# Moving two small table loads from the store queue to the load queue, behind the first data tile

## The chip, the cores and the metric

The kernel runs on one core of a Trainium2 chip. The metric is the device time of one execution in microseconds (us), as a median of several executions. A profile of one execution gives a "span", from the first to the last of the program's own instructions, which is here about 1.8 us shorter than the time. Executions more than 1.5% above the fastest of the same kernel are called slow; the others are called fast.

A DMA is a transfer between the chip's main memory and the on-chip buffers. It is issued on a queue (the texts also say ring) and carried out in packets, one record each in the trace, by sixteen DMA engines that both queues of this kernel use. It has landed when a counter, its semaphore, has been raised sixteen times; "semaphore records" are the times of these raises.

A ratio below is the mean time of one kernel's fast runs over the mean of the other's fast runs of the same rounds. It is therefore not quite the ratio of the medians that are quoted next to it.

## The reference

A rotary embedding is applied to the first half of the last axis; the second half is passed through.

```python
# x: (16, 512, 16, 64) float32; cos, sin: (512, 32) float32
x1, x2 = x[..., :32], x[..., 32:]
c, s = cos[None, :, None, :16], sin[None, :, None, :16]      # only the first 16 columns are used
first  = x1[..., :16] * c - x1[..., 16:] * s
second = x1[..., :16] * s + x1[..., 16:] * c
out = concatenate([first, second, x2], axis=-1)
```

x is 33.55 MB and is read once and written once. Each table is 64 KB.

## The kernel before

x is cut into T = 8 tiles of 128 partitions by 8192 values (32 KB per partition, 4.19 MB per tile). A tile is loaded on the queue of the sync engine (SP), rotated in place by VectorE, and stored on the queue of ScalarE (ACT). Five x buffers exist, so load t+5 must wait until store t has landed. The two tables are loaded at the start on the store queue, into 64 partitions, and four small copies spread them over 128 partitions.

```python
    stage = const_pool.tile([PB, 2, K, HF], fp32)
    nc.scalar.dma_start(out=stage[:, 0].rearrange("p k j -> p (k j)"), in_=cosf)   # 64 KB
    nc.scalar.dma_start(out=stage[:, 1].rearrange("p k j -> p (k j)"), in_=sinf)   # 64 KB

    table = const_pool.tile([P, 2, K, 2, Q], fp32)
    for r in range(REP):            # 2
        for t in range(2):          # cos, sin
            nc.vector.tensor_copy(out=table[r * PB : (r + 1) * PB, t], in_=stage[:, t, ...])
    ...
    KC = 4
    for t in range(T):              # 8 tiles
        x_t = x_pool.tile([P, K, H, D], fp32)          # 5 buffers
        nc.sync.dma_start(out=x_t..., in_=xf[t])       # 4.19 MB
        for k0 in range(0, K, KC):                     # two halves
            ...
            nc.vector.tensor_mul(out=a_t[:], in0=x1, in1=c)
            nc.vector.tensor_mul(out=b_t[:], in0=x1, in1=s)
            nc.vector.tensor_sub(out=x1[:, :, :, 0:Q], ...)
            nc.vector.tensor_add(out=x1[:, :, :, Q:HF], ...)
        nc.scalar.dma_start(out=of[t], in_=x_t...)     # 4.19 MB
```

Of the kernel before, what the change touches and what calls it, by code (L numbers as in the profile page):

```python
# [1 line left out]

# [4 lines left out]


@with_exitstack
def kernel(  # L10
    ctx: ExitStack,
    tc: tile.TileContext,
    x: bass.AP,
    cos: bass.AP,
    sin: bass.AP,
    out: bass.AP,
):
    nc = tc.nc
    fp32 = mybir.dt.float32
    P = 128  # L20
    B, S, H, D = x.shape
    Q = D // 4
    HF = D // 2


    K = 8
    T = B * S // (P * K)
    PB = S // K
    REP = P // PB

    xf = x.rearrange("b s h d -> (b s h d)").rearrange("(t p f) -> t p f", t=T, p=P)
    of = out.rearrange("b s h d -> (b s h d)").rearrange("(t p f) -> t p f", t=T, p=P)
    cosf = cos.rearrange("(p k) j -> p (k j)", k=K)
    sinf = sin.rearrange("(p k) j -> p (k j)", k=K)

    const_pool = ctx.enter_context(tc.tile_pool(name="const", bufs=1))
    x_pool = ctx.enter_context(tc.tile_pool(name="xp", bufs=5))
    ab_pool = ctx.enter_context(tc.tile_pool(name="abp", bufs=1))

    stage = const_pool.tile([PB, 2, K, HF], fp32)  # L40
    nc.scalar.dma_start(out=stage[:, 0].rearrange("p k j -> p (k j)"), in_=cosf)  # L41
    nc.scalar.dma_start(out=stage[:, 1].rearrange("p k j -> p (k j)"), in_=sinf)


    table = const_pool.tile([P, 2, K, 2, Q], fp32)
    for r in range(REP):
        for t in range(2):
            nc.vector.tensor_copy(  # L48
                out=table[r * PB : (r + 1) * PB, t],
                in_=stage[:, t, :, 0:Q].unsqueeze(2).to_broadcast((PB, K, 2, Q)),  # L50
            )
    C = table[:, 0].rearrange("p k c j -> p k (c j)")
    Sn = table[:, 1].rearrange("p k c j -> p k (c j)")

    KC = 4
    for t in range(T):
        x_t = x_pool.tile([P, K, H, D], fp32)
        nc.sync.dma_start(out=x_t.rearrange("p k h d -> p (k h d)"), in_=xf[t])  # L58
        for k0 in range(0, K, KC):
            x1 = x_t[:, k0 : k0 + KC, :, 0:HF]  # L60
            c = C[:, k0 : k0 + KC].unsqueeze(2).to_broadcast((P, KC, H, HF))
            s = Sn[:, k0 : k0 + KC].unsqueeze(2).to_broadcast((P, KC, H, HF))
            a_t = ab_pool.tile([P, KC, H, HF], fp32)
            b_t = ab_pool.tile([P, KC, H, HF], fp32)
            nc.vector.tensor_mul(out=a_t[:], in0=x1, in1=c)  # L65
            nc.vector.tensor_mul(out=b_t[:], in0=x1, in1=s)  # L66
            nc.vector.tensor_sub(  # L67
                out=x1[:, :, :, 0:Q], in0=a_t[:, :, :, 0:Q], in1=b_t[:, :, :, Q:HF]
            )
            nc.vector.tensor_add(  # L70
                out=x1[:, :, :, Q:HF], in0=a_t[:, :, :, Q:HF], in1=b_t[:, :, :, 0:Q]
            )
        nc.scalar.dma_start(out=of[t], in_=x_t.rearrange("p k h d -> p (k h d)"))


# [1 line left out]
_INS = ['x', 'cos', 'sin']  # L77
_OUTS = [((16, 512, 16, 64), 'float32')]


# [23 lines left out]
```

## Time and profile before

| | before |
|---|---|
| time, median of the first 3 runs | 162.37 us (162.19 to 162.39) |
| span in the profile | 160.4 us |
| VectorE busy | 110.8 us (69%) |
| moved by DMA | 67.25 MB, mean 419 GB/s |
| one 32 KB packet on one DMA engine (packet records) | 1.213 us, on either queue |

The profile's page of the kernel before: span, busy time of VectorE (DVE), and strips of 40 slices of 4 us each, in which a digit is the busy share in tenths.

```profile
span 160.4 us, 155 instructions
DVE 110.8 (69%) x68; POOL 0.2 (0%) x4
DVE  0001599999999999999998799609995099940000
DMA  7999999999999999999999999999999999999993
DMA packets 2465, 67.25 MB, mean 419 GB/s; under 512 B 288, under 2 KB 416, under 8 KB 416
```

DMA is at 9 from the second slice to the last but one. VectorE is idle in the first three slices, has holes late, and is done four slices before the end. Sixteen engines at 32,768 B per 1.213 us move 432 GB/s, and 67.2 MB at 432 GB/s take 155.6 us. That is nearly the whole span.

The timeline of the kernel before (start us, duration us, engine and line, operation, count; in brackets the idle time before and what ended it; SPq and ACTq are the sequencers that issue DMAs):

```profile
0.73 0.54 ACTq L41 DMA_DIRECT2D stage<-in_cos_dram  x1
0.73 11.78 SPq L58 DMA_DIRECT2D x_t<-in_x_dram  x5
1.30 0.61 ACTq L42 DMA_DIRECT2D stage<-in_sin_dram  x1
...
12.19 0.59 DVE L48 COPY table<-stage 64x256 f32<-64x256 f32 x2 [12.19 <-DMA stage<-in_cos_dram]
17.67 0.59 DVE L48 COPY table<-stage 64x256 f32<-64x256 f32 x2 [4.90 <-DMA stage<-in_sin_dram]
18.29 2.29 DVE L65 TENSOR_TENSOR a_t<-x_t,table 128x2048 f32<-128x2048 f32 x1
...
32.14 0.35 ACTq L73 DMA_DIRECT2D out_dram<-x_t  x1
```

Two 64 KB loads issued at 0.73 and 1.30 us hold VectorE up until 12.19 and 17.67 us. X tile 0 landed at 13.62 us (semaphore records), so 18.29 us is 4.7 us later than the data would allow. This is what the change is after.

The waits of the kernel before (who waited for what: us in total, number of waits, longest):

```profile
DVE a_t L65 <- DMA x_t<-in_x_dram: 13.2, 3, 5.9
DVE table L48 <- DMA stage<-in_cos_dram: 12.2, 1, 12.2
DVE table L48 <- DMA stage<-in_sin_dram: 4.9, 1, 4.9
```

The chain of work that ended last, of the kernel before (start us, us, what), cut to its two long links:

```profile
59.83 34.11 DMA out_dram<-x_t
...
93.99 34.21 DMA x_t<-in_x_dram
```

A store takes 34 us from issue to landing, and the load that waits for its buffer takes 34 us more. One tile alone takes 9.7 us at 432 GB/s (4.19 MB / 432 GB/s); the rest is standing in queues that are never empty.

### The profile page before, as it was taken

What the parts mean: (1) busy time and instruction counts of PE and PEld (TensorE: products, weight loads), DVE (VectorE), ACT (ScalarE), POOL (GpSimd) and SP (SyncE); (2) the same over time, 40 slices, a digit from 0 to 9 for tenths busy, and PEclk for the clock granted to TensorE, in tenths of its full rate; (3) what the DMA queues carried; (4) which work ended last, traced back from release to release, by engine and by line L of the source; (5) the groups of instructions that cost most, each with busy time, mean ns of one, the idle gap of its engine ahead of it and who ended that gap; (6) DMA issues with size and microseconds to landing.
All of it is one profiled execution on the core that took longest, in us unless ns stands there. A gap on an engine that the chain in (4) does not pass through costs nothing.

```text
span 160.4 us, 155 instructions
## 1 busy us (share of the span) xinstructions
DVE 110.8 (69%) x68; POOL 0.2 (0%) x4
## 2 busy tenths in 40 slices
DVE  0001599999999999999998799609995099940000
POOL 0000000000000000000000000000000000000000
DMA  7999999999999999999999999999999999999993
GB/s 253 408 400 408 392 417 490 400 408 498 400 400 474 433 392 457 457 392 449 466 392 417 490 400 408 498 400 400 476 425 400 466 441 400 449 457 400 417 482 147
DMA packets 2465, 67.25 MB, mean 419 GB/s; under 512 B 288, under 2 KB 416, under 8 KB 416
## 3 DMA queue, kind: packets, MB, share of 16 engines
q1 hardware_dynamic: 1152, 33.55, 49.3%
q10 hardware_dynamic: 1312, 33.69, 48.7%
q14 instruction: 1, 0.01, 0.0%
HBM read 33.69 MB, written 33.55 MB: 419 GB/s over the span
## 4 chain that ended last, share of the span: by engine, by line
DMA 53%; DVE 30%; issue 4%; DVEq 1%; ACTq 0%; SPq 0%
DMA x_t<-in_x_dram 21%; DMA out_dram<-x_t 21%; DVE b_t L66 11%; DMA stage<-in_sin_dram 10%; DVE a_t L65 10%; DVE x_t L70 5%; DVE x_t L67 4%; DVEq L99 1%; ACTq L41 0%; DVE table L48 0%; SPq L58 0%; DVEq L65 0%
## 5 line engine op out<-in xcount | busy, mean ns | idle before, releaser
L65 DVE TENSOR_TENSOR a_t<-x_t,table 128x2048 f32<-128x2048 f32 x16 | 36.7, 2292 | 13.6 <-DMA x_t<-in_x_dram 13.2
L66 DVE TENSOR_TENSOR b_t<-x_t,table 128x2048 f32<-128x2048 f32 x16 | 36.5, 2284 | 0.0
L67 DVE TENSOR_TENSOR x_t<-a_t,b_t 128x1024 f32<-128x1024 f32 x16 | 19.6, 1226 | 0.6
L70 DVE TENSOR_TENSOR x_t<-a_t,b_t 128x1024 f32<-128x1024 f32 x16 | 19.5, 1218 | 0.0
L48 DVE COPY table<-stage 64x256 f32<-64x256 f32 x4 | 1.1, 287 | 17.1 <-DMA stage<-in_cos_dram 12.2
L88 POOL MEMSET const-bfloat16-1.0<- 128x1 bf16 x1 | 0.1, 102 | 0.0
L88 POOL MEMSET const-uint8-127<- 128x1 uint8 x1 | 0.1, 102 | 0.0
L88 POOL MEMSET const-float32-0.0<- 128x1 f32 x1 | 0.1, 99 | 0.2 <-issue 0.2
L88 POOL MEMSET const-float32-1.0<- 128x1 f32 x1 | 0.1, 99 | 0.0
## 6 DMA issues: line engine op xcount, KB each, us to landing
x_t<-in_x_dram SPq DMA_DIRECT2D x8, 4096.0 KB, 33.9
out_dram<-x_t ACTq DMA_DIRECT2D x8, 4096.0 KB, 31.3
stage<-in_cos_dram ACTq DMA_DIRECT2D x1, 64.0 KB, 11.4
stage<-in_sin_dram ACTq DMA_DIRECT2D x1, 64.0 KB, 16.3
```

The lines of the kernel that those rows point to most:

```text
L48: nc.vector.tensor_copy(out=table[r * PB : (r + 1) * PB, t], in_=stage[:, t, :, 0:Q].unsqueeze(2).to_broadcast((PB, K, 2, Q)),)
L65: nc.vector.tensor_mul(out=a_t[:], in0=x1, in1=c)
L66: nc.vector.tensor_mul(out=b_t[:], in0=x1, in1=s)
L67: nc.vector.tensor_sub(out=x1[:, :, :, 0:Q], in0=a_t[:, :, :, 0:Q], in1=b_t[:, :, :, Q:HF])
L70: nc.vector.tensor_add(out=x1[:, :, :, Q:HF], in0=a_t[:, :, :, Q:HF], in1=b_t[:, :, :, 0:Q])
L88: nc = _bacc.Bacc("TRN2", target_bir_lowering=False, num_devices=1)
L99: with _tile.TileContext(nc) as tc:
```

## The change

Its intent: load x tile 0 first, put the tables right behind it on the same queue, and so let VectorE begin as soon as tile 0 is there.

```diff
+    x_0 = x_pool.tile([P, K, H, D], fp32, name="x_t")
+    nc.sync.dma_start(out=x_0.rearrange("p k h d -> p (k h d)"), in_=xf[0])
+
     stage = const_pool.tile([PB, 2, K, HF], fp32)
-    nc.scalar.dma_start(out=stage[:, 0].rearrange("p k j -> p (k j)"), in_=cosf)
-    nc.scalar.dma_start(out=stage[:, 1].rearrange("p k j -> p (k j)"), in_=sinf)
+    nc.sync.dma_start(out=stage[:, 0].rearrange("p k j -> p (k j)"), in_=cosf)
+    nc.sync.dma_start(out=stage[:, 1].rearrange("p k j -> p (k j)"), in_=sinf)
 ...
     for t in range(T):
-        x_t = x_pool.tile([P, K, H, D], fp32)
-        nc.sync.dma_start(out=x_t.rearrange("p k h d -> p (k h d)"), in_=xf[t])
+        if t == 0:
+            x_t = x_0
+        else:
+            x_t = x_pool.tile([P, K, H, D], fp32, name="x_t")
+            nc.sync.dma_start(out=x_t.rearrange("p k h d -> p (k h d)"), in_=xf[t])
```

## The prediction

> **What bounds the kernel.** DMA, nearly from end to end. The page's DMA view gives 67.25 MB at a mean of 419 GB/s over the 160.4 us span; in its strip of 40 slices DMA stands at 9 in all but the first and last. In the packet records a 32 KB packet takes 1.213 us on either queue; 16 engines then move 432 GB/s, and 67.2 MB take 155.6 us. First packet 1.7 us, last 159.2: under 2 us is lost. VectorE is busy 110.8 us (69%). The chain of waits starts with 16.3 us of "DMA stage<-in_sin" and VectorE work, but from 59.8 us it is store, load: full queues.
>
> **What the change does.** The same bytes move. The two 64 KB table loads leave the store queue (ScalarE) for the load queue (SP), behind x tile 0. Before, cos was issued at 0.73 us and landed at 12.16, sin at 17.65, although a 1 KB packet itself takes 46 ns. The Trainium skill, "DMA: Bandwidth & Descriptors", section "Queues, rings and completion order", says each engine round-robins between queues at packet granularity. The trace agrees: 4 data packets and a completion per engine took 6.2 us (5.95 to 12.16), five turns of 1.24 us, each behind one 32 KB packet of x. In one ring behind x tile 0, the tables pass together.
>
> Costed: x tile 0 landed at 13.6 us with the tables taking turns; without them about 13.0. Both tables should land by about 13.3. Two copies (0.6 us), first multiply about 13.9 (before: 18.29). The sin copies now sit between the first two multiplies (by the order of instructions). First store issued at about 28.3 us instead of 32.14: VectorE gains about 4 us.
>
> **How much is critical.** Almost nothing. I replayed the transfers as two first-in-first-out queues that share 432 GB/s equally when both have work, five x buffers, 13.85 us of VectorE per tile. With the old start this gives the old landings within 1 us. With the start 4 us earlier, early stores take bandwidth from loads sooner: tile 3 lands at about 54 us (before 50.4), the last load at about 132 (before 128.2). The last store is issued at about 146 instead of 142.1, still about 2 us before the previous store has drained, so DMA never runs dry: the end stays at about 159.4. The early microseconds come back as VectorE waiting for x.
>
> Small terms: the table turns cost about 0.6 us of DMA throughput between 6 and 18 us (bytes by 20 us against 432 GB/s); small packets in a row in the load ring may cost as much, or up to 1 us.
>
> **Prediction:** 162.2 us, range 161.3 to 163.4 (8 in 10). Faster by over 2%: 0.02. Within 2%: 0.96. Slower by over 2%: 0.02.
>
> **What would show the steps.** Cos, sin and x tile 0 landing within 1 us of each other, at 12.5 to 14.5 us. First store near 28 us. DMA strip still 9 throughout. VectorE busy still about 110.8 us; its wait for the tables shrinks to about zero; its wait for x rises from 13.2 us in 3 waits to about 33 (13 before the first tile, then four of 4 to 6). Last load lands 3 to 5 us later, last store issued near 146 us, landing near 159.
>
> **What would make it wrong.** DMA running dry at the end, if the last load lands after about 134 us (up to 1.5 us slower); small packets stalling the load ring by microseconds; a changed reuse of DMA semaphores that delays a load; a rate that differs between pure and mixed traffic, since the pure-load stretch shortens.

## The result, and the profile after

| first measurement | before | after |
|---|---|---|
| median of all 6 runs | 162.28 us | 162.73 us |
| range | 162.16 to 162.77 | 162.20 to 175.38 |
| ratio of the fast runs | | 1.0005 (95%: 0.9981 to 1.003) |

The fast runs are the same. Two of the six runs of the changed kernel were slow (172.58 and 175.38 us), and its first profile fell into one of these. The profile shown here as "after" is therefore that of a second measurement of the identical kernel (after_again, 162.25 us, a fast run).

The page of the changed kernel in a fast run:

```profile
span 160.5 us, 154 instructions
DVE 110.8 (69%) x68; POOL 0.2 (0%) x4
DVE  0005999999999999957997099950999319993000
DMA  7999999999999999999999999999999999999993
DMA packets 2465, 67.25 MB, mean 419 GB/s; under 512 B 288, under 2 KB 416, under 8 KB 416
```

The DMA strip is the same, digit for digit. VectorE's strip has a 5 instead of a 1 in the fourth slice, where it starts, and its holes come earlier and are one more.

The timeline of the changed kernel in the same run:

```profile
0.73 0.36 SPq L41 DMA_DIRECT2D x_t<-in_x_dram  x1
1.14 0.53 SPq L44 DMA_DIRECT2D stage<-in_cos_dram  x1
1.72 0.58 SPq L45 DMA_DIRECT2D stage<-in_sin_dram  x1
...
13.65 0.59 DVE L51 COPY table<-stage 64x256 f32<-64x256 f32 x2 [13.65 <-DMA stage<-in_cos_dram]
14.27 2.29 DVE L71 TENSOR_TENSOR a_t<-x_t,table 128x2048 f32<-128x2048 f32 x1
16.48 0.58 DVE L51 COPY table<-stage 64x256 f32<-64x256 f32 x2
...
28.74 0.38 ACTq L79 DMA_DIRECT2D out_dram<-x_t  x1
```

The change does what it intends. X tile 0, cos and sin land at 13.38, 13.63 and 13.93 us, the first multiply starts 4.0 us earlier, and the first store goes out 3.4 us earlier (28.74 against 32.14; the sin copies now stand between the first two multiplies).

The waits of the changed kernel:

```profile
DVE a_t L71 <- DMA x_t<-in_x_dram: 20.3, 4, 6.1
DVE table L51 <- DMA stage<-in_cos_dram: 13.7, 1, 13.7
```

VectorE waited 12.2 + 4.9 = 17.1 us at the start before, and 13.7 us now: 3.4 us saved. It waited 13.2 us for later x tiles before, and 20.3 us now: 7.1 us lost. So VectorE ends its last tile 3.7 us later than before, and the kernel is not slower only because the store queue was still busy with the store before, as the landing times below show.

The chain of the changed kernel, the same two links:

```profile
56.44 33.63 DMA out_dram<-x_t
...
90.12 41.74 DMA x_t<-in_x_dram
```

The store is issued 3.4 us earlier and lands 3.9 us earlier, so the last load is issued 3.9 us earlier (90.12 against 93.99). But that load then takes 41.7 us instead of 34.2, because more of the load queue is still ahead of it: it lands at 131.86 us, 3.7 us **later** than before (128.20).

All of this is seen at once in the landing times, read from the semaphore records of the two traces (us):

```
                          before   after (fast)
first store issued         32.14      28.74
x tile 2 landed            33.43      34.49
x tile 3 landed            50.43      53.86
x tile 4 landed            69.78      73.20
x tile 7 landed (last)    128.20     131.86
last store issued         142.14     145.80
store before it landed    149.95     149.97
last store landed         159.59     159.61
```

Until the first store's packets (from 36.03 us before, from 32.39 us after), the load queue has the DMA engines alone, apart from the tables. From then on, as long as there are loads, the two queues share them about half each in the packet records of both traces (50% and 50% before, 51% and 49% after). A store that starts 3.4 us earlier takes its share from the loads about as much sooner. The order of the bytes changes; their sum and the rate do not.

### The profile page after: what moved, and what is told of

It is laid out like the page before. It is cut to its first block, busy times and chain, and to the rows that moved or that the text cites. A ratio compares the mean times of both kernels' runs of the same rounds, so it can differ in the third digit from the quotient of the medians.

```text
span 170.8 us, 154 instructions
## 1 busy us (share of the span) xinstructions
DVE 110.8 (65%) x68; POOL 0.2 (0%) x4
## 4 chain that ended last, share of the span: by engine, by line
DMA 57%; DVE 29%; issue 3%; DVEq 1%; SPq 0%
DMA out_dram<-x_t 25%; DMA x_t<-in_x_dram 24%; DVE b_t L72 10%; DVE a_t L71 9%; DMA stage<-in_cos_dram 7%; DVE x_t L76 5%; DVE x_t L73 4%; DVEq L105 1%; DVE table L51 0%; SPq L41 0%; SPq L64 0%; DVEq L71 0%
## 5 line engine op out<-in xcount | busy, mean ns | idle before, releaser
L51 DVE COPY table<-stage 64x256 f32<-64x256 f32 x4 | 1.1, 284 | 13.9 <-DMA stage<-in_cos_dram 13.9
```

## The experiments

Theory A is the one of the prediction: the transfers are a fixed 67.2 MB at about 432 GB/s, and VectorE's head start only moves stores ahead of loads. Four rivals are tested along with it: the head start is real and is eaten by the table packets in the load ring (B); an earlier start can never hurt (C); the start of VectorE is critical, microsecond for microsecond; the end of the kernel is bound by its last tile.

### after_again: the changed kernel once more

No edit.

> The changed kernel again, unedited, to get a profile of an undisturbed execution (the first one was of the slow state) and to count slow executions of both kernels. Theory A (the transfers are a fixed 67.2 MB at about 432 GB/s, and a head start of VectorE only reorders loads and stores): 162.0 to 162.6 us in fast runs, first store issued at 29 us, last load landing at 132 to 133, last store issued at 146 to 147, DMA never idle until 159. Rival B (the head start is real and is eaten by the table packets in the load ring): the same total, but x tiles 1 and 2 landing some 4 us later than before, and a DMA strip with a hole near 12 to 16 us.

Measured: fast runs 162.25 to 162.60 us, ratio 0.9997 (0.9982 to 1.0012), and one slow run of 168.55 in five. Its profile is the one shown above. X tile 1 landed at 23.50 us (before 23.73) and x tile 2 at 34.49 (33.43), so the 4 us that rival B expects to be lost between 12 and 35 us are not lost there. Each number of theory A came out within 1 us.

### no_tables: the tables' traffic taken away

```diff
-    nc.sync.dma_start(... in_=cosf)
-    nc.sync.dma_start(... in_=sinf)
-    for r in range(REP): ...tensor_copy(out=table[...], in_=stage[...])
+    nc.vector.memset(table[:], 1.0)          # wrong result on purpose
```

> The tables are filled with a constant by VectorE instead of being loaded (wrong result on purpose). First multiply at about 13.4 us, when x tile 0 lands. Theory A: only the table traffic goes, 0.3 us of bytes and up to 0.5 us of bubble: 0.3 to 0.8 us faster than before, 161.5 to 162.0. Rival B (table packets in the load ring eat about 4 us): 157.5 to 159 us.

Measured: 162.47 us, ratio 1.0005 (0.9992 to 1.0018). Rival B falls: without any table packets nothing is gained, and the 1.2 us found below is too little for its 4 us. But the expectation of A was missed as well, by 0.3 to 0.8 us. The packet records tell where that went. With each packet's bytes spread over its duration, DMA moved, in GB/s by stretches of 5 us (432 is full; rows and columns are our own sums):

```
us from start       5-10  10-15  15-20  20-25  25-30  30-35  35-40
before               427    396    419    431    432    432    433
after (fast)         433    389    432    432    432    427    434
no_tables            433    433    433    433    398    361    433
no_tables_warm       430    426    432    432    417    380    433
no_tables_delay      433    433    433    433    433    414    402
```

Before, the tables cost throughput in turns from 5 to 20 us; after, in one piece at 10 to 15 us: (432 - 389) x 5 us = 0.2 MB, or 0.5 us. Without tables this loss is gone. In its place load packets of 1.4 to 2.7 us instead of 1.213 appear from 28 to 33 us, about the time of the first store: (34 + 71) x 5 us = 0.5 MB, or 1.2 us. The saving (0.3 us of table bytes and 0.5 us of loss) was spent there.

### early and early_split: an even earlier start

```diff
+    # early: tables first, then x tile 0 in two half loads
     nc.sync.dma_start(... in_=cosf)
     nc.sync.dma_start(... in_=sinf)
-    nc.sync.dma_start(out=x_0..., in_=xf[0])
+    for k0 in range(0, K, 4):
+        nc.sync.dma_start(out=x_0[:, k0 : k0 + 4]..., in_=xf[0][:, k0 * H * D : (k0 + 4) * H * D])
 ...
+    # early_split: in addition the last tile's store in two halves, each as soon as it is computed
+            if t == T - 1:
+                nc.scalar.dma_start(out=of[t][:, k0 * H * D : (k0 + KC) * H * D], in_=x_t[:, k0 : k0 + KC]...)
```

> Tables at the head of the load queue and x tile 0 in two half loads, so that VectorE starts at 8 to 10 us and the first store goes out at about 24 us instead of 29. Theory A: the loads fall back further behind the stores, the last load lands at about 137, the last store is issued at about 151 while the store before has drained at 148.6: DMA is idle for 2.5 to 4 us and the kernel gets slower, 164.5 to 166.5 us. Rival C (an earlier start cannot hurt, at worst it is absorbed): 162.0 to 162.6 us or less.

> As early, and the store of the last tile goes out in two halves, the first as soon as its half is computed. Theory A: the hole before the last store is filled by the first half, back to 162.0 to 162.8 us. If early was slower for another cause than the hole at the end (the split load of x tile 0, the tables in front): no recovery, 164.5 or more.

Measured: early 166.95 us, ratio 1.0272 (1.0245 to 1.0298); early_split 163.79 us, ratio 1.0089 (1.0073 to 1.0106). Both lie above their ranges of theory A, by 0.5 and 1.0 us. Early missed on the side away from rival C. Early_split missed towards its rival (no recovery, 164.5 us or more): of the 4.5 us that early lost, 3.2 came back, so the hole at the end is most of the loss and not all of it. VectorE starts 4.7 us earlier than in the changed kernel (9.59 against 14.27), and the kernel becomes 2.7% slower than before. Rival C falls. The last load of early lands at 139.12 us and its last store is issued at 153.06, after the store before it had landed (151.20).

The windows view shows the hole (window, its length, busy time of VectorE and count, of GpSimd, the TensorE clock, DMA share, GB/s; a packet counts whole in the window in which it starts, so a share can be over 1). First the changed kernel in a fast run:

```profile
145.00:150.00 5.00, 0.77 (x1) 0.00 (x0) 1.00 1.03 446
150.00:155.00 5.00, 0.00 (x0) 0.00 (x0) 1.00 1.08 465
```

Then early:

```profile
145.00:150.00 5.00, 4.97 (x3) 0.00 (x0) 1.00 0.94 406
150.00:155.00 5.00, 2.99 (x3) 0.00 (x0) 1.00 0.24 105
```

Then early_split:

```profile
145.00:150.00 5.00, 4.97 (x4) 0.00 (x0) 1.00 1.00 433
150.00:155.00 5.00, 3.14 (x3) 0.00 (x0) 1.00 0.98 419
```

In early, DMA is at 24% from 150 to 155 us, while VectorE works on the last tile: nothing is left to move. The first half of the last store fills this hole in early_split and wins back 3.2 us. The 1.4 us that remain over before are the start: with the tables in front, DMA had moved 0.5 MB by 5 us instead of 1.0 MB (1.15 us), and packets were slow about the first store here too (0.8 us); the 0.5 us of the table loss are saved.

### behind_x1, behind_x2, behind_x3: a later start

The tables stand behind x tiles 0 to 1, 0 to 2, or 0 to 3 on the load queue.

```diff
     nc.sync.dma_start(out=x_0..., in_=xf[0])
+    nc.sync.dma_start(out=x_1..., in_=xf[1])        # behind_x1
+    nc.sync.dma_start(out=x_2..., in_=xf[2])        # behind_x2, with the line above
+    nc.sync.dma_start(out=x_3..., in_=xf[3])        # behind_x3, with both
     nc.sync.dma_start(... in_=cosf)
     nc.sync.dma_start(... in_=sinf)
```

> The change with one more x tile ahead of the tables: x tiles 0 and 1, then the tables. First multiply at about 24 us, ten later than in the changed kernel and six later than before. Theory A (VectorE's start is off the critical path within a band): 162.0 to 162.8 us, last load landing at about 123, last store issued at about 137, DMA never idle. A rival that takes the start of VectorE for critical (each us of start is a us of time): 172 us.

> Tables behind x tiles 0 to 2, first multiply at about 34 us. Theory A: the five x buffers are full at about 53 us and the first store, issued at 49 us, has not landed: the load queue waits until about 64, the store queue is alone and has a gap, DMA is idle for about 2 us: 164 to 165.5 us. Start critical: 182 us. Start free at any place: 162.4.

> Tables behind x tiles 0 to 3, first multiply at about 44 us. Theory A: now VectorE's 111 us of work and the ends on either side set the time, DMA is idle for about 11 us: 172 to 175 us. Start critical: 192 us. Start free: 162.4.

Measured, with the start experiment of above, in the order of VectorE's start (first multiply and first store from the profiles; the profile of behind_x1 is slow, its times here lie before the disturbance):

| kernel | first multiply, us | first store issued, us | fast runs, us | ratio to before |
|---|---|---|---|---|
| early | 9.59 | 23.43 | 166.31 to 167.19 | 1.0272 |
| after | 14.27 | 28.74 | 162.25 to 162.60 | 0.9997 |
| before | 18.29 | 32.14 | 162.20 to 162.77 | 1 |
| behind_x1 | 24.11 | 38.58 | 162.20 and 162.33 | 0.9992 |
| behind_x2 | 34.02 | 48.48 | 165.33 to 165.76 | 1.0196 |
| behind_x3 | 43.59 | 58.05 | 172.26 to 173.61 | 1.0652 |

Over a band of about 10 us of VectorE's start (14 to 24 us) the time does not move by more than 0.1% (the last point has two fast runs only). Earlier and later it gets worse, for two reasons that can be seen. The strips of behind_x2:

```profile
DVE  0000000089999999999999999999999999950000
DMA  7999899989999986999989999999999999999993
```

and of behind_x3:

```profile
DVE  0000000000999999999999999999999999990000
DMA  7999999989990298799999999898999999998993
```

When the start is late, VectorE has no holes any more, and the holes move into the DMA strip: in behind_x2 at 61 to 65 us (the digit 6), in behind_x3 at 51 to 60 us (the digits 0 and 2), where the five buffers are full and the first store has not landed. From 45 to 85 us DMA fell short of 432 GB/s by 3.3 us' worth of bytes in behind_x2 and 10.2 us' in behind_x3 (packet records, our own sums; none in before and after). The medians grew by 3.2 and 11.0 us over before. Both "start critical" (182 and 192 us) and "start free at any place" (162.4) fall. Behind_x2 came out 0.1 us above its range.

### after_split: is the end bound by the last tile?

The changed kernel with the last store in halves, as in early_split.

> The changed kernel with the last tile's store in two halves. Theory A: in fast runs the last store is already issued 3 us before the store ahead of it has drained, there is no hole to fill, so nothing is gained: 162.0 to 162.8 us. If the end of the changed kernel were bound by the last tile (load, compute, store), the half store would win 3 to 7 us.

Measured: fast runs 162.26, 162.36 and 162.97 us, ratio 1.0009 (0.999 to 1.0029); three of six runs were slow (172.20 to 175.27). In fast runs there is nothing to gain, as expected where the queue is not yet empty when the last store is issued. The same edit won 3.2 us in early.

### half_store2: fewer bytes

```diff
+        if t == 2:                                   # half of tile 2 is never stored (wrong result)
+            nc.scalar.dma_start(out=of[t][:, 0 : 4 * H * D], in_=x_t[:, 0:4]...)
+        elif t < T - 1:
```

> after_split with only half of tile 2 stored (wrong result on purpose): 2.1 MB less to move in the middle of the kernel, VectorE's work and all starts unchanged. Theory A: 2.1 MB at 432 GB/s, 4.85 us faster than after_split: 157.0 to 158.2 us. If something other than DMA throughput bounds the middle (VectorE, the buffers' turnaround): 160 us or more.

Measured: fast runs 157.55 to 157.79 us (one slow run of 163.66), ratio to before 0.9709 (0.9695 to 0.9723). Against the fast runs of after_split this is 162.36 - 157.61 = 4.75 us, where 2.1 MB at 432 GB/s are 4.85 us. From the page of half_store2:

```profile
span 156.0 us, 155 instructions
DVE 110.8 (71%) x68; POOL 0.2 (0%) x4
DMA packets 2609, 65.15 MB, mean 418 GB/s; under 512 B 304, under 2 KB 432, under 8 KB 432
```

VectorE's work is unchanged and the mean rate is the same (418 GB/s against 419). This is the only edit that made the kernel clearly faster, and it did so by moving fewer bytes. Half a store also lands sooner and frees its buffer sooner; but in the packet records DMA moved 429 to 434 GB/s in every 5 us from 15 to 145, so it was the bytes, not a wait for a buffer, that filled the time.

### no_tables_warm and no_tables_delay: the slow stretch about the first store

```diff
+    # no_tables_warm: no_tables, and one unused 64 KB load on the store queue at the start
+    nc.scalar.dma_start(out=stage.rearrange("p k j -> p (k j)"), in_=cosf)
```

```diff
+            # no_tables_delay: no_tables, and 4.6 us of needless work before the first tile
+            if t == 0 and k0 == 0:
+                for _ in range(2):
+                    nc.vector.tensor_mul(out=a_t[:], in0=x1, in1=c)
```

> no_tables was expected 0.3 to 0.8 us faster and was not: its load packets took about 2 us instead of 1.21 from 28 to 33 us, about the first store, and cost some 1.2 us of throughput. In the kernel before, the store queue had carried the tables at its start and no such stretch is seen. This kernel is no_tables with one 64 KB load (unused) on the store queue at the start. Theory W (the first use of the store queue costs a warm-up, which falls on full traffic when the tables are not on it): the slow stretch is gone, 161.4 to 162.1 us. If the stretch has another cause: still there at 27 to 33 us, 162.4 us or more.

> no_tables with two needless multiplies (4.6 us) before the first tile, so that the first store goes out at about 31.5 us, as in the kernel before (wrong result on purpose). Theory D (the slow stretch of load packets at 28 to 33 us in no_tables goes with the first store starting early, within x tile 2): no slow stretch, and the 0.3 to 0.8 us that the tables' traffic costs become visible: 161.4 to 162.0 us, although VectorE starts later. If the stretch is there whatever the time of the first store: 162.3 us or more.

Measured: no_tables_warm 162.47 us, ratio 1.0007 (0.9994 to 1.0019); the slow stretch is still there (table under no_tables: 15 + 52 below 432, about 0.8 us). Theory W falls: that the store queue had been used before does not prevent it.

No_tables_delay: 162.10 us, ratio 0.9988 (0.9974 to 1.0002), 0.1 us above its range. The stretch moved with the first store, from 28 to 33 us to 34 to 37 us, and shrank to about half: (18 + 30) x 5 us = 0.24 MB, or 0.6 us. So it goes with the first store in these traces, but issuing that store nearly as late as before (31.38 against 32.14 us) does not remove it: theory D is right in part only. Before shows no such stretch and after hardly any (5 x 5 us, 0.06 us). What sets its size is open. Starting VectorE 4.6 us of useless work later made this kernel 0.4 us faster than no_tables, by the medians; the intervals of the two ratios overlap, so this gain is not clear of noise.

### after_count, and the slow executions

No edit.

> The changed kernel a third time. So far 3 of its 12 executions, and 2 of 4 of behind_x1, were slow (166 to 175 us), and none of over 20 of the kernel before. Theory A says nothing of this. If slow executions are chance on any kernel, some of before's should show them as well by now, and few here; if the change makes them likelier, again about one in four here and none of before. Fast runs: 162.1 to 162.7 us.

(The text counts 12 executions where there were 11 of the unchanged after kernel by then.)

Measured: fast runs 162.19 to 162.83 us, ratio 1.0003 (0.9987 to 1.0018), and two of six runs slow (174.58 and 175.88). Over the study the changed kernel was slow in 5 of 17 executions and the kernel before in 0 of 35. If slowness fell on the 52 executions at random, all five would fall on the changed kernel with a chance of about 0.0024 (17·16·15·14·13 / 52·51·50·49·48). That count includes the runs that raised the question, and takes executions as independent. After_count alone, which was run to test it, has 2 of 6 against 0 of 11, for which the chance is 0.11 (6·5 / 17·16). That the change makes slow executions likelier is therefore probable, not shown. (The first measurement's list of runs has a seventh execution of the changed kernel, a fast one of 162.22 us, that its summary leaves out.) Of the other kernels, behind_x1 was slow in 2 of 4, after_split in 3 of 6, half_store2 in 1 of 4; the other seven in 0 of 32, two of them (behind_x2, behind_x3) also with the tables between x tiles on the load queue.

What a slow execution looks like can be said. From the page of the changed kernel in a slow run (172.58 us):

```profile
DMA  7999898989899999999999989898999999706960
```

At the end the strip has the digits 7, 0 and 6 where a fast run has 9. The sixteen DMA engines report each transfer's end one by one. For the third store, in time order (us):

```
fast run:  89.7 89.7 89.7 89.8 89.8 89.8 89.8 89.9 89.9 89.9 89.9 90.0 90.0 90.0 90.1 90.1
slow run:  89.7 89.8 89.8 89.8 89.9 89.9 90.0 90.0 90.0 90.1 90.1 90.1 90.1 90.1 90.2 100.2
```

Fifteen engines are on time and one is 10 us behind. The Trainium skill, "DMA: Bandwidth & Descriptors", section "Why a DMA increments its semaphore by 16 and not by 1", says that a DMA runs on up to 16 engines that finish independently and that only the full count means the data has landed. The trace agrees: the load that waited for this store was issued at 100.22 us instead of 90.12. The packet records show what the lag is made of: from 41 us on, about every 3 us one store packet took 1.3 to 1.9 us, together 8.8 us over 1.213 each by 100.2 us, while between 36 and 130 us no store packet of the fast run took over 1.25. The slow profile of behind_x1 shows two engines behind in this way, that of after_split five. Why these packets are slow, and why these kernels meet it and the kernel before did not, no run here shows. It is left open.

## Why the prediction was right

Point by point, against the fast profile of the changed kernel:

| step of the prediction | predicted | measured |
|---|---|---|
| time | 162.2 us (161.3 to 163.4) | 162.73 us median of all; fast runs 162.2 to 163.0 |
| x tile 0 lands | 13.0 | 13.38 |
| both tables land | by 13.3 | 13.63, 13.93 |
| first multiply | 13.9 | 14.27 |
| first store issued | 28.3 | 28.74 |
| x tile 3 lands | 54 | 53.86 |
| last load lands | 132 | 131.86 |
| last store issued | 146 | 145.80 |
| last store lands | 159.4 | 159.61 |

- **DMA throughput bounds the kernel.** Shown by half_store2: 2.1 MB less took 4.75 us off, at unchanged VectorE work and with DMA full throughout.
- **The head start is given back as waits for x.** Shown by the waits (13.2 us in 3 before, 20.3 us in 4 after), and by the landing times. Over the kernels, an earlier first store goes with a later x tile 3: it lands at 61.04 us for a store at 23.43 (early), 54.92 at 26.89 (no_tables), 53.86 at 28.74 (after), 50.43 at 32.14 (before), 44.17 at 38.58 (behind_x1); no_tables_warm (55.06 at 27.28) and no_tables_delay (49.73 at 31.38) are out of this order by 0.1 and 0.7 us. In early the waits outgrew the margin at the end: it lost 4.5 us (166.95 - 162.41), 3.2 us of them in the hole at the end and the rest at the start. The replay that gave the prediction's landing times is not in the record; that they came out within 0.4 us is what speaks for it.
- **The end stays fed.** The last store is issued 7.8 us before the store ahead of it lands in the kernel before (149.95 - 142.14) and 4.2 us before it after the change (149.97 - 145.80). A part of that distance is the landing itself, since the last packets end before the landing is told, so the margin is smaller still; early had used it up. Our estimate from the packet records: the store before had its last packet done at 149.53 us, and early's last store, on an empty queue, took 0.84 us from issue to its first packet, which leaves about 2.9 us. The estimate of the prediction was 2 us.
- **Mis-sized terms.** X tile 0 gained 0.24 us (13.62 to 13.38) instead of 0.6. In no_tables it landed at 12.94, where the prediction had put it, so the tables delay the tile's landing by 0.44 us even from behind it. In the packet records sixteen 32 KB packets, as many as there are engines, took 1.57 to 1.71 us instead of 1.213 at 12.4 to 13.0 us. The prediction allowed for a loss of this kind; it measured 0.5 us, about what the turns had cost before.
- **A misread line.** "Its wait for the tables shrinks to about zero" did not come out as such: the view puts the first 13.7 us down to cos, which landed 0.25 us after x tile 0. The sum was right (33 predicted, 20.3 + 13.7 = 34.0 measured).
- **What the prediction did not see:** the slow executions, in 5 of 17 runs of the changed kernel. The range held the median of all runs in the first measurement, but with some luck: two of the six were slow, and with three, as in after_split, the median of all came to 167.59 us. The mechanism is borne out by the fast runs alone, and a user would meet 168 to 176 us in some executions.

No version beats both kernels. The best with a right result are before, after, after_split and behind_x1, with fast runs of 162.1 to 163.0 us, and before alone of these showed no slow run.

## What to carry to other kernels

With the DMA strip full from end to end, an earlier start of the compute engine was worth nothing here: ask not when work can begin but whether the DMA engines will run empty, because lost DMA time and bytes were what cost. With loads and stores sharing the engines, an early store pushed later loads back, so the head start ate the margin at the end, and past a point (here between a first multiply at 14.3 and at 9.6 us) it made the kernel slower; splitting the last store won most of that back (3.2 of 4.5 us). Before taking a change that leaves the time the same, count the slow executions over many runs too, not the medians alone.

## What the Trainium skill lacked or had wrong

- "DMA: Bandwidth & Descriptors", "Queues, rings and completion order" states the round-robin between queues but not what it costs a small transfer: beside a queue of 32 KB packets, 4 data packets and a completion per engine took five turns of 1.24 us, and a 64 KB load 11.4 us from issue to landing; behind x tile 0 in the same queue, the landing came 0.25 us after the tile's.
- Same page, "SWDGE vs HWDGE vs iDMA" gives a packet as preferably at most 4096 B, but in the table on the software queue (SWDGE), and no page read gives a size in bytes for packets of the hardware queues used here; the records of these transfers show packets of 32,768 B, one row of a partition each, and the turns had about their length (1.24 us against 1.213).
- Same page, "Where 436 GB/s comes from" says that about 358 GB/s bind transfers between HBM and SBUF, although it also names a measured 425 GB/s. This kernel, on one core, moved 430 to 434 GB/s in every 5 us from 25 to 150 us in the kernel before, with loads, stores, or both. "HBM Reference", "Specifications (TRN2)", is closer: about 425 GB/s for a core that streams alone.
- No page read has the slow stretch about the first store on a loaded queue (load packets of 1.4 to 2.7 us instead of 1.213, 0 to 1.2 us lost in all, depending on the kernel).
- No page read has DMA engines that fall behind in some executions of a kernel only, as seen here: one, two or five of the sixteen up to 12 us behind the others in the three slow profiles, with slow executions in 5 of 17 of one kernel and 0 of 35 of another that moves the same bytes.
